# Hybrid S5 / conv / mLSTM layer on one core: the sixteen copies of the S5 inputs become steps of the S5 side job

## The chip, the cores and the metric

The kernel runs on 1 core of one Trainium2 chip. The metric is the device time of one execution in microseconds (us). The kernel before takes 1469.58 us (median of 3 runs, 1468.60 to 1469.86).

## What is computed

One layer of a diffusion backbone (`DEPTH = 1`) on 256 latent tokens with a prefix of 256 context tokens, both 2048 wide. Both streams are normalised and modulated, go through one input projection, and feed three groups of heads; their outputs are concatenated, projected and followed by a SwiGLU feed-forward block.

```python
hx = _rmsnorm(x, norm1_g[l]) * (1.0 + sc1_x) + sh1_x
hc = _rmsnorm(ctx, norm1_g[l]) * (1.0 + sc1_c) + sh1_c
zx = hx @ w_in[l] + b_in[l]
zc = hc @ w_in[l] + b_in[l]
s5_c, s5_x = s5_mixer(zc[..., OFF_S5:OFF_CONV], zx[..., OFF_S5:OFF_CONV], ...)
ml_c, ml_x = mlstm_mixer(zc, zx, ml_norm_g[l], need_ctx)
cv_x = conv_module(zx[..., OFF_CONV:OFF_Q], ...)
x = x + g1_x * (jnp.concatenate([s5_x, cv_x, ml_x], axis=-1) @ w_out[l])
hx2 = _rmsnorm(x, norm2_g[l]) * (1.0 + sc2_x) + sh2_x
x = x + g2_x * _swiglu(hx2, w_ffn_in[l], w_ffn_out[l])
```

The change concerns the input of `s5_mixer`. It has 32 groups of 16 channels, each with a state of 64 complex numbers, scanned along the tokens in both directions. The input is the S5 part of `zc` and `zx`, 512 channels by 512 tokens.

## The kernel before

**The main stream.** TensorE multiplies the weights of the input projection, the GLU, the output projection and the feed-forward block, one chunk after the other. A chunk is 8 weight tiles of 128 by 128 in fp32. SyncE fetches it (`raw`, line 259), ScalarE rounds it (`whi`, a CAST by `acopy`, line 201), and VectorE takes the rest (`wlo = raw - whi`, line 168). There are three buffers of each. A tile is used in three matmuls for each output (`mm3`: whi by high part, whi by low part, wlo by high part, line 208), so a chunk with one moving block of 256 tokens is 24 matmuls of 256 columns. The order of the tiles is fixed by `tile_order()`: S5 and the first K tiles, then the conv tiles (where the change acts), the other K tiles, V, Q, O, and so on.

**The side jobs.** All other work is written as generators which the class `Sched` steps between tiles. It holds three counters (`sc.pe`, `sc.dve`, `sc.act`), to which the helpers add an estimated cost; every 8 tiles `pump()` steps the ready job with the lowest priority number until VectorE or ScalarE is counted more than 3500 ns ahead of TensorE. A step may return a delay. The S5 job and the conv job have priority 3, the modulation job (`mod_job`: matrix-vector products with the `wm` weights, whose sums are `macc` and `mods`) 2, the gates of the mLSTM 1 and its heads 4. The framework then settles the order in which each engine gets its instructions, engine by engine, and adds the waits.

**The S5 job.** The four tiles of its input come out of the main stream as `zT` (channels by tokens). Sixteen copies (`s5_moves`, lines 773 to 781) bring them into chunk layout `U`: each copies 32 partitions by 512 elements, eight on ScalarE and eight on VectorE, alternating. They are issued in one block, ahead of the job (line 925). The job then runs 16 rounds. `prep(p)` builds the tables of round p: `Wb`, `Mb` and `cc` from the parameters, the rotation table `tab` on ScalarE, four transposes of `Wb` (line 839) whose result ScalarE copies to `Wi`, and 16 matmuls `Mb` by `Wb` whose result ScalarE copies to `M2`. `main5(p)` multiplies `U[:, p, :]` by `Wi`, rotates and scans on VectorE (`Vr`), forms `H1`, and multiplies `H1` by `Mb` and `U` by `M2`; VectorE adds the result into `U`. `prep(p + 1)` and `main5(p)` are interleaved step by step. After round 15 ScalarE applies the GELU to `U` (line 907), and 32 copies bring it into `gT`, sixteen of them on ScalarE.

**PSUM.** The main stream has three banks `m` and two banks `qk`. All side jobs and conv tile 0 share three banks `b` (`bbank`): a side job that needs a bank waits until the reader of its last use is done. Lines 992 and 994 are the transposes at the end of the gates job, line 749 those of the modulation sums, line 755 the sums of these on ScalarE, line 187 those on VectorE (`rsum`).

Of the kernel before, what the change touches and what calls it, by code (L numbers as in the profile page):

```python
# [150 lines left out]
def hybrid_layer_kernel(ctx: ExitStack, tc: tile.TileContext, xt, ctxt, wm1, wmr, wst, wg, bvrow, pvd, cstd, s5p, out):  # L151
# [6 lines left out]
    sc = Sched()  # L158


    def n_of(ap):
        n = 1
        for s in ap.shape[1:]:
            n *= s
        return n

    def tt(o, a, b, op):
        V.tensor_tensor(out=o, in0=a, in1=b, op=op)  # L168
        sc.dve += 62 + 1.05 * n_of(o)
# [8 lines left out]
    def stt(o, a, s, b, op0, op1):  # L178
        V.scalar_tensor_tensor(o, a, s, b, op0=op0, op1=op1)  # L179
        sc.dve += 62 + 1.05 * n_of(o)  # L180

    def vcopy(o, a):
        V.tensor_copy(o, a)
        sc.dve += 62 + 0.8 * n_of(o)
# [5 lines left out]
    def scan(o, d0, d1, init, op0, op1):  # L190
        V.tensor_tensor_scan(o, d0, d1, init, op0=op0, op1=op1)
        sc.dve += 62 + 1.05 * n_of(o)
# [7 lines left out]
    def acopy(o, a):  # L200
        S.copy(o, a)  # L201
        sc.act += 190 + 0.84 * n_of(o)

    def mm(o, l, r, start, stop, native=False, tp=None, sgc=False, pin=False):
        kw = {}
        if tp is not None:
            kw["tile_position"] = tp
        i = P.matmul(o, lhsT=l, rhs=r, start=start, stop=stop, skip_group_check=sgc, **kw)  # L208
        if pin:
            tc.keep_in_program_order(i)  # L210
        n = n_of(o)
        sc.pe += (max(n * 4, 512) if native else max(n, 256)) / 2.36 / (1 if tp is None else 4)
# [10 lines left out]
    def bbank():  # L223
        return bank("b", 3)

    def tmp(n=512):
        return sb.tile([128, 512], F32, name="tmp", tag="tmp", bufs=4)[:, :n]
# [9 lines left out]
    def pvc(name, i=0, n=None):  # L237
        a, w = PV[name]
        return pv[:, a + i:a + i + (n if n is not None else 1)]
# [374 lines left out]
    zT = pre.tile([128, 4, 512], F32, name="zT", tag="T1")  # L614
# [155 lines left out]


    U = pre.tile([128, 16, 128], F32, name="U", tag="U")
    def s5_moves():
        for s in range(4):
            for q in range(4):
                o = U[32 * s:32 * s + 32, q::4, :]
                i = zT[32 * q:32 * q + 32, :, s::4]
                if (s + q) % 2:
                    vcopy(o, i)
                else:  # L780
                    acopy(o, i)

    def s5_job():
        Wb = pre.tile([128, 2, 2, 4, 32], F32, name="Wb", tag="s5W")
# [70 lines left out]
        def main5(p):  # L855
            u0 = 2 * p
            Mb, Wi, M2, tab = P5.pop(p)
            ps = bbank()
            pv4 = ps.rearrange("p (u r k) -> p u r k", u=2, r=2)
            for d in range(2):  # L860
                r = U[:, p, :]
                if d:
                    r = r.rearrange("p (h k) -> p h k", h=2)[:, :, ::-1]
                for ri in range(2):
                    mm(pv4[:, d, ri, :], Wi[:, d, ri, :], r, True, True, native=True)
            Vr = pre.tile([128, 2, 2, 128], F32, name="Vr", tag="s5V")
            P2 = tmp().rearrange("p (u r k) -> p u r k", u=2, r=2)
            tt(Vr, pv4, tab[:, :, 0:1, :].to_broadcast([128, 2, 2, 128]), OP.mult)
            tt(P2, pv4[:, :, ::-1, :], tab[:, :, 1:2, :].to_broadcast([128, 2, 2, 128]), OP.mult)
            tt(Vr[:, :, 0, :], Vr[:, :, 0, :], P2[:, :, 0, :], OP.add)  # L870
            tt(Vr[:, :, 1, :], Vr[:, :, 1, :], P2[:, :, 1, :], OP.subtract)
            yield
            for d in range(2):
                for ri in range(2):
                    scan(Vr[:, d, ri, :], rho[:, u0 + d:u0 + d + 1].to_broadcast([128, 128]), Vr[:, d, ri, :],
                         0.0, OP.mult, OP.add)
            yield
            H1 = tmp(256).rearrange("p (u r k) -> p u r k", u=2, r=2)
            H2 = tmp(256).rearrange("p (u r k) -> p u r k", u=2, r=2)
            tt(H1, Vr[:, :, :, 63:127], tab[:, :, 0:1, 63:127].to_broadcast([128, 2, 2, 64]), OP.mult)  # L880
            tt(H2, Vr[:, :, ::-1, 63:127], tab[:, :, 1:2, 63:127].to_broadcast([128, 2, 2, 64]), OP.mult)
            tt(H1[:, :, 0, :], H1[:, :, 0, :], H2[:, :, 0, :], OP.subtract)
            tt(H1[:, :, 1, :], H1[:, :, 1, :], H2[:, :, 1, :], OP.add)
            yield S5_Y[3]
            ps = bbank()
            for d in range(2):
                for ri in range(2):
                    h = H1[:, d, ri, :]
                    mm(ps[:, 0:64], Mb[:, d, ri, (1 - d):(5 - d), :].rearrange("p s c -> p (s c)"),
                       h[:, ::-1] if d else h, d == 0 and ri == 0, False, native=True)  # L890
            mm(ps[:, 0:64], M2, U[:, p, 64:128], False, True, native=True)
            stt(U[:, p, 64:128], U[:, p, 64:128], pvc("dcol", p), ps[:, 0:64], OP.mult, OP.add)
            yield

        yield from prep(0)
        for p in range(16):
            a, b = main5(p), (prep(p + 1) if p < 15 else iter(()))
            live = [b, a]
            while live:
                for g in list(live):  # L900
                    try:
                        d = next(g)
                    except StopIteration:
                        live.remove(g)
                        continue
                    yield
# [3 lines left out]
        for hh in range(2):  # L910
            for j in range(4):
                for q in range(4):
                    o, i = gT[hh][32 * q:32 * q + 32, :, j::4], U[32 * j:32 * j + 32, q + 8 * hh:q + 8 * hh + 5:4, 64:128]
# [8 lines left out]
            tt(gs[:, 2 * hh:2 * hh + 2, 1, :], gT[hh], gs[:, 2 * hh:2 * hh + 2, 0, :], OP.subtract)  # L922
        s5o["gT"], s5o["gs"] = gT, gs

    s5_moves()
    s5o = {}
    s5j = sc.add(s5_job(), P_S5)


# [364 lines left out]
    i = 0  # L1294
# [114 lines left out]
```

## Time and profile before

| What | Value |
|---|---|
| median of 3 runs | 1469.58 us (1468.60 to 1469.86) |
| time of the profiled execution | 1469.76 us |
| its span, first to last instruction | 1468.0 us |
| TensorE busy | 1423.0 us, 97% of the span |
| VectorE, ScalarE, GpSimdE busy | 68%, 49%, 7% |
| mean granted clock of TensorE | 0.991 |
| chain that ended last, by engine | PE 87%, DVE 4%, ACT 3%, DMA 2%, issue 2% |

PE is TensorE, PEld its weight load, DVE is VectorE, ACT is ScalarE, POOL is GpSimdE and SP is SyncE. A row of a timeline has the start and the duration in us, the engine, the line, the operation and its tiles; "xN" counts records, and a square bracket gives the idle time before it and what ended that. A matmul with fp32 operands leaves two records. The shares are means over the span; what a stage loses is read from its own rows.

### The profile page before, as it was taken

To read this page: it belongs to the slowest core of one execution; us is meant where nothing else is said; L and a number is where in the kernel's file an instruction comes from. 1 tells how busy PE (TensorE), PEld (TensorE's weight loads), DVE (VectorE), ACT (ScalarE), POOL (GpSimd) and SP (SyncE) were. 2 spreads that over 40 slices of the span, in tenths; PEclk is the share of its full clock that TensorE was granted. 3 is DMA by queue.
4 is the path that set the end of the run, shared out by engine and by line. 5 is a ranking of instruction groups with operands and counts; after the bars stand their busy time and mean duration, and the time that the engine had idled before them with its cause. 6 is when DMAs were issued, how large, how long until landed. Compare 5 with 4: busy or idle time off the path is not lost.

```text
span 1468.0 us, 29243 instructions
## 1 busy us (share of the span) xinstructions
PE 1423.0 (97%) x11840; PEld 1335.7 (91%) x11840; DVE 1004.2 (68%) x1960; ACT 716.0 (49%) x1199; POOL 107.2 (7%) x207
## 2 busy tenths in 40 slices
PE   6999899999999999998999999999999999999996
PEld 3888788887878999998999999999999999999996
DVE  7655699998988787988776667555544554555554
ACT  4333786654656555545544444433444334443353
POOL 1221111110101011111010000000000000000000
PEclk9999999999999999999999999999999999999999
DMA  9997464443436576688477786555555555555553
GB/s 359 360 360 294 160 234 138 165 162 123 147 121 233 196 270 237 239 312 321 150 262 269 257 291 237 186 187 187 185 184 185 186 188 182 186 187 187 186 175 114
DMA packets 87943, 315.56 MB, mean 215 GB/s; under 512 B 10096, under 2 KB 10880, under 8 KB 87808
## 3 DMA queue, kind: packets, MB, share of 16 engines
q1 hardware_dynamic: 60912, 216.67, 42.9%
q0 software_dynamic: 26896, 97.02, 18.4%
q8 instruction: 93, 1.52, 0.4%
q14 instruction: 42, 0.34, 0.1%
HBM read 311.55 MB, written 2.10 MB: 214 GB/s over the span
## 4 chain that ended last, share of the span: by engine, by line
PE 87%; DVE 4%; ACT 3%; DMA 2%; issue 2%; SPq 0%; POOL 0%; DVEq 0%; POOLq 0%; ACTq 0%
PE ps_m L208 71%; PE ps_b L208 11%; PE ps_qk L208 4%; DMA wm<-in_wm_dram 1%; DVE tmp L168 1%; DMA tmp<-in_wg_dram 1%; DVE macc L179 1%; DMA raw<-in_wst_dram 1%; DVE wlo L168 1%; PE ps_b L839 0%; ACT whi L201 0%; ACT tmp L195 0%; ACT U L201 0%; PE ps_b L749 0%; DVE xres L168 0%
## 5 line engine op out<-in xcount | busy, mean ns | idle before, releaser
L168 DVE TENSOR_TENSOR wlo<-raw,whi 128x1024 fp32r<-128x1024 f32 x386 | 471.9, 1224 | 315.9 <-ACT whi L201 311.1
L201 ACT CAST whi<-raw 128x1024 fp32r<-128x1024 f32 x386 | 404.0, 1047 | 502.3 <-PE ps_m L208 355.9
L208 PE MATMUL ps_m<-h,whi 128*128 128x256 f32 x2624 | 469.9, 282 | 3.6 <-ACT h L195 3.6
L208 PEld LDWEIGHTS ps_m<-h,whi 128*128 128x128 f32 x2624 | 403.8, 189 | 4.0 <-ACT h L195 4.0
L208 PE MATMUL ps_m<-h,wlo 128*128 128x256 f32 x1312 | 369.6, 282 | 0.0
L208 PE MATMUL ps_m<-ffa,whi 128*128 128x256 f32 x1408 | 251.1, 281 | 0.0
L208 PEld LDWEIGHTS ps_m<-h,wlo 128*128 128x128 f32 x1312 | 247.5, 189 | 0.0
L208 PEld LDWEIGHTS ps_m<-ffa,whi 128*128 128x128 f32 x1408 | 215.7, 188 | 1.4 <-issue 1.2
L208 PE MATMUL ps_m<-ffa,wlo 128*128 128x256 f32 x704 | 197.3, 280 | 0.0
L208 PE MATMUL ps_m<-hx,whi 128*128 128x256 f32 x960 | 186.9, 290 | 5.5 <-ACT hx L195 3.6
L208 PEld LDWEIGHTS ps_m<-hx,whi 128*128 128x128 f32 x960 | 148.8, 190 | 24.7 <-issue 16.3
L179 DVE SCALAR_TENSOR_TENSOR macc<-wm,cs,macc 128x512 f32<-128x512 f32 x180 | 134.6, 748 | 6.8 <-ACT macc L195 5.1
L208 PE MATMUL ps_m<-hx,wlo 128*128 128x256 f32 x480 | 135.5, 283 | 0.4 <-DVE wlo L168 0.4
L208 PEld LDWEIGHTS ps_m<-ffa,wlo 128*128 128x128 f32 x704 | 132.2, 188 | 0.0
L331 POOL DMA_DIRECT2D wm<-in_wmr_dram x128 | 67.5, 528 | 606.8 <-DVE macc L179 429.8
L208 PEld LDWEIGHTS ps_m<-hx,wlo 128*128 128x128 f32 x480 | 90.9, 190 | 0.8 <-DVE wlo L168 0.8
L179 DVE SCALAR_TENSOR_TENSOR xres<-ps_m,mods,xres 128x256 f32<-128x256 f32 x96 | 46.1, 482 | 35.2 <-PE ps_m L208 35.0
L179 DVE SCALAR_TENSOR_TENSOR XB<-XB,pv 128x256 f32<-128x256 f32 x120 | 53.9, 481 | 0.6
L208 PE MATMUL ps_m<-hc,whi 128*128 128x256 f32 x256 | 52.9, 288 | 0.0
L208 PE MATMUL ps_m<-mixm,whi 128*128 128x256 f32 x256 | 47.0, 285 | 0.0
L208 PE MATMUL ps_m<-whi,hx 128*128 128x512 f32 x128 | 46.5, 400 | 0.0
L201 ACT CAST ffa<-tmp 128x256 fp32r<-128x256 f32 x44 | 17.7, 405 | 49.7 <-DVE tmp L168 49.7
(267 smaller groups left out, 1967.2 us busy)
## 6 DMA issues: line engine op xcount, KB each, us to landing
raw<-in_wst_dram SPq DMA_DIRECT2D x386, 512.0 KB, 3.5
wm<-in_wmr_dram POOLq DMA_DIRECT2D x128, 512.0 KB, 5.4
wm<-in_wm_dram POOLq DMA_DIRECT2D x32, 512.0 KB, 7.2
wmu<-in_wm_dram POOLq DMA_DIRECT2D x16, 512.0 KB, 7.2
wmt<-in_wm_dram POOLq DMA_DIRECT2D x7, 512.0 KB, 5.9
wm<-in_wm_dram SPq DMA_DIRECT2D x5, 512.0 KB, 10.2
xr<-in_xt_dram SPq DMA_DIRECT2D x4, 512.0 KB, 6.5
cr<-in_ctxt_dram SPq DMA_DIRECT2D x4, 512.0 KB, 9.0
```

The costliest lines, as they stand in the source:

```text
L168: V.tensor_tensor(out=o, in0=a, in1=b, op=op)
L179: V.scalar_tensor_tensor(o, a, s, b, op0=op0, op1=op1)
L201: S.copy(o, a)
L208: i = P.matmul(o, lhsT=l, rhs=r, start=start, stop=stop, skip_group_check=sgc, **kw)
L331: i = (q or nc.gpsimd).dma_start(wm[key], src)
```

## The change

The function `s5_moves`, which issued all sixteen copies, becomes the generator `s5_move(q)`. It issues the four copies of quarter q (the rounds p = q, q + 4, q + 8, q + 12 take their input from it), two on ScalarE and two on VectorE, adds 500 to the counter `sc.act` for each copy on ScalarE, and returns to the planner after each two copies. The S5 job runs quarter 0 ahead of `prep(0)`, and quarters 1, 2 and 3 ahead of rounds 0, 1 and 2. Lines of the S5 job stand two lower in the kernel after, later ones four lower.

```diff
--- before.py
+++ after.py
@@ -770,15 +770,17 @@
 
 
     U = pre.tile([128, 16, 128], F32, name="U", tag="U")
-    def s5_moves():
+    def s5_move(q):
         for s in range(4):
-            for q in range(4):
-                o = U[32 * s:32 * s + 32, q::4, :]
-                i = zT[32 * q:32 * q + 32, :, s::4]
-                if (s + q) % 2:
-                    vcopy(o, i)
-                else:
-                    acopy(o, i)
+            o = U[32 * s:32 * s + 32, q::4, :]
+            i = zT[32 * q:32 * q + 32, :, s::4]
+            if (s + q) % 2:
+                vcopy(o, i)
+            else:
+                acopy(o, i)
+                sc.act += 500
+            if s % 2:
+                yield
 
     def s5_job():
         Wb = pre.tile([128, 2, 2, 4, 32], F32, name="Wb", tag="s5W")
@@ -892,8 +894,11 @@
             stt(U[:, p, 64:128], U[:, p, 64:128], pvc("dcol", p), ps[:, 0:64], OP.mult, OP.add)
             yield
 
+        yield from s5_move(0)
         yield from prep(0)
         for p in range(16):
+            if p < 3:
+                yield from s5_move(p + 1)
             a, b = main5(p), (prep(p + 1) if p < 15 else iter(()))
             live = [b, a]
             while live:
@@ -922,7 +927,6 @@
             tt(gs[:, 2 * hh:2 * hh + 2, 1, :], gT[hh], gs[:, 2 * hh:2 * hh + 2, 0, :], OP.subtract)
         s5o["gT"], s5o["gs"] = gT, gs
 
-    s5_moves()
     s5o = {}
     s5j = sc.add(s5_job(), P_S5)
```

The instructions of the kernels are the same in number and kind but for two table loads on ScalarE fewer; their order differs. Until conv tile 0 has begun (some 151 us in the trace of before) and from 600 us on, each engine has the same order in both. Three places between follow.

The first is ScalarE at the beginning of the conv tiles. Before, the one copy and the block of seven copies to `U` stand ahead of the CASTs of the weight chunks:

```order
L201 COPY U_1768<-zT_1744 32x4x128
L195 ACTIVATE kT_1749<-ps_b_221,bks_1750 128x512
L195 ACTIVATE kT_1749<-ps_b_222,bks_1750 128x512
L201 COPY U_1768<-zT_1744 32x4x128 x7
L201 CAST whi_1818<-raw_1786 128x1024
L201 CAST whi_1866<-raw_1816 128x1024
L201 COPY Mb_1833<-tmp_1922 64x20x16
L201 CAST whi_1896<-raw_1864 128x1024
L195 ACTIVATE tmp_1932<-cst_68,s5c_215 128x128
```

After, the copies are spread. The row `Wi` is the copy that frees the PSUM bank of the first four transposes of `Wb`, and `M2` the one behind the first `Mb` by `Wb` matmuls; this is what stands ahead of them:

```order
L195 ACTIVATE cc_2020<-bc_2002 128x2x16
L195 ACTIVATE cc_2020<-bc_2002 128x64
L201 COPY U_1768<-zT_1744 32x4x128
L195 ACT_TABLE_LOAD
L195 ACTIVATE tab_1889<-tmp_1890 128x2x128
L195 ACTIVATE tmp_1891<-tmp_1890 128x256
L201 CAST whi_1926<-raw_1852 128x1024
L195 ACTIVATE tab_1889<-tmp_1891,kc_70 128x2x128
L201 CAST whi_1998<-raw_1924 128x1024
L201 COPY Wi_1938<-ps_b_1939 128x512
L201 COPY U_1768<-zT_1744 32x4x128 x3
L201 COPY M2_1945<-ps_b_1946 128x128
```

Two CASTs now stand ahead of the six last copies, and those copies ahead of the later CASTs, of `Wi` and of `M2`. VectorE's eight copies stay one block at their place.

The second is VectorE in the gates job, from the first scans of the forget gate to the row that the gate transposes (line 992, after: 996) read. Before:

```order
L191 SCALAR_TENSOR_TENSOR tmp_2894<-kc_70,tmp_2892 32x256 x4
L168 TENSOR_TENSOR wlo_3116<-raw_2967,whi_3114 128x1024
L168 TENSOR_TENSOR rows_2839<-rows_2839,tmp_2894 64x512
L168 TENSOR_TENSOR tmp_2984<-tmp_2984,tmp_2985 128x256
L173 TENSOR_SCALAR rows_2839<-rows_2839,tmp_2894 32x256 x2
L191 SCALAR_TENSOR_TENSOR tmp_2893<-kc_70,tmp_2894,rows_2839 32x256 x2
L191 SCALAR_TENSOR_TENSOR tmp_2893<-kc_70,tmp_2893,rows_2839 32x256 x2
L179 SCALAR_TENSOR_TENSOR XB_1755<-XB_1755,pv_64 128x256
L173 TENSOR_SCALAR tmp_2893<-tmp_2893 64x256
L179 SCALAR_TENSOR_TENSOR XB_1755<-XB_1755,pv_64 128x256
L168 TENSOR_TENSOR rows_2839<-tmp_2893,tmp_2894 64x256
```

After, with a step of the modulation job next to it; the row `mods` frees the PSUM bank of a modulation sum:

```order
L191 SCALAR_TENSOR_TENSOR tmp_2801<-kc_70,tmp_2799 32x256 x4
L179 SCALAR_TENSOR_TENSOR XB_1755<-XB_1755,pv_64 128x256
L168 TENSOR_TENSOR rows_2773<-rows_2773,tmp_2801 64x512
L179 SCALAR_TENSOR_TENSOR XB_1755<-XB_1755,pv_64 128x256
L173 TENSOR_SCALAR rows_2773<-rows_2773,tmp_2801 32x256 x2
L191 SCALAR_TENSOR_TENSOR tmp_2800<-kc_70,tmp_2801,rows_2773 32x256 x2
L191 SCALAR_TENSOR_TENSOR tmp_2800<-kc_70,tmp_2800,rows_2773 32x256 x2
L168 TENSOR_TENSOR tmp_2830<-tmp_2830,tmp_2831 128x256
L173 TENSOR_SCALAR tmp_2800<-tmp_2800 64x256
L187 TENSOR_REDUCE mods_1759<-ps_b_2936 128x4
L168 TENSOR_TENSOR rows_2773<-tmp_2800,tmp_2801 64x256
```

The sum of the modulation job stands behind the second scans, and on TensorE the transposes of the gates, which in the kernel after take the bank that this sum reads, stand behind it.

The third is ScalarE at the end of the S5 job, where the V tiles end and the Q tiles begin (`RH` is the Q tile with its bias that the heads need). Before:

```order
L201 CAST whi_5475<-raw_5429 128x1024
L195 ACT_TABLE_LOAD
L195 ACTIVATE U_1768<-U_1768 128x16x64
L201 COPY gT_5336<-U_1768 32x128 x8
L201 COPY gT_5337<-U_1768 32x128 x8
L201 CAST whi_5505<-raw_5473 128x1024
L201 CAST gs_5400<-gT_5336 128x2x256
L201 CAST gs_5400<-gT_5337 128x2x256
L201 CAST whi_5537<-raw_5503 128x1024
L201 CAST whi_5575<-raw_5535 128x1024
L195 ACTIVATE RH_5471<-ps_m_5472,pv_64 128x256
```

After:

```order
L201 CAST whi_5532<-raw_5481 128x1024
L195 ACT_TABLE_LOAD
L195 ACTIVATE U_1768<-U_1768 128x16x64
L755 ACTIVATE macc_4921,mods_1759<-ps_b_5487 128x128
L201 COPY gT_5382<-U_1768 32x128 x8
L201 COPY gT_5383<-U_1768 32x128 x8
L755 ACTIVATE macc_4921,mods_1759<-ps_b_5487 128x128
L201 CAST gs_5446<-gT_5382 128x2x256
L201 CAST gs_5446<-gT_5383 128x2x256
L755 ACTIVATE macc_4921,mods_1759<-ps_b_5487 128x128 x2
L195 ACTIVATE RH_5479<-ps_m_5480,pv_64 128x256
L195 ACTIVATE macc_5497<-wm_5281,cs_104 128x512
```

Before, the last matmuls of round 15 (`U` by `M2`) stand 21 matmuls ahead of the end of the V tiles on TensorE; after, they stand two matmuls ahead of it. The GELU, the copies to `gT` and the CASTs to `gs` now stand between the CAST of the third chunk of Q (`whi_5532`) and `RH`, with the CASTs of the fourth and fifth chunk behind `RH`. Before, the CASTs of three more chunks stood ahead of `RH`.

## Rows read from the trace of the kernel before

**Rows 1.** waits of TensorE, 140 to 450 us: us, times, longest

```profile
PE ps_b L208 <- ACT whi L201: 4.1, 1, 4.1
```

**Rows 2.** the timeline of TensorE, 155 to 182 us

```profile
159.23 0.80 PE L208 MATMUL ps_b<-hx,whi 128*128 128x256 f32 x2 [4.07 <-ACT whi L201]
...
171.38 1.06 PE L208 MATMUL ps_b<-wm,cs 128*32 128x512 f32 x6
172.38 0.66 PE L839 MATMUL ps_b<-cst,Wb 128*128 128x128 f32 x4
172.96 0.89 PE L208 MATMUL ps_b<-Mb,Wb 128*32 128x128 f32 x32
...
174.12 1.05 PE L208 MATMUL ps_b<-U,Wi 128*128 128x128 f32 x8
...
181.70 1.08 PE L208 MATMUL ps_b<-tmp,Mb 128*128 128x64 f32 x8
```

**Rows 3.** the timeline of ScalarE, 146 to 176 us

```profile
150.29 7.82 ACT L201 COPY U<-zT 32x512 f32<-32x512 f32 x7
158.14 1.99 ACT L201 CAST whi<-raw 128x1024 fp32r<-128x1024 f32 x2
...
163.23 1.28 ACT L195 ACT_TABLE_LOAD   x1
...
173.07 0.59 ACT L201 COPY Wi<-ps_b 128x512 f32<-128x512 f32 x1 [0.64 <-PE ps_b L839]
173.88 0.27 ACT L201 COPY M<-ps_b 128x128 f32<-128x128 f32 x1 [0.22 <-PE ps_b L208]
```

**Rows 4.** windows: length, busy times, then the granted clock

```profile
158.00:159.00 1.00, 0.00 (x0) 0.00 (x0) 0.00 (x0) 0.97 (x2) 0.00 (x0) 0.50 0.00 0
160.15:167.10 6.95, 6.95 (x38) 5.29 (x37) 3.48 (x5) 6.50 (x13) 0.00 (x0) 0.72 0.66 225
245.00:250.00 5.00, 5.00 (x30) 4.80 (x30) 4.87 (x10) 2.51 (x5) 0.00 (x0) 0.66 0.18 71
450.00:455.00 5.00, 3.42 (x22) 2.83 (x23) 5.00 (x8) 1.48 (x3) 0.53 (x1) 1.00 0.55 181
```

**Rows 5.** the timeline of VectorE, 146 to 184 us

```profile
147.58 5.00 DVE L183 COPY U<-zT 32x512 f32<-32x512 f32 x8 [1.78 <-ACT zT L195]
```

**Rows 6.** the timeline of TensorE, 229 to 245 us

```profile
231.49 1.12 PE L208 MATMUL ps_b<-rows,XB 32*128 32x512 f32 x2
...
244.02 0.30 PE L992 MATMUL ps_b<-cst,rows 64*128 64x64 f32 x2 [1.44 <-DVE rows L168]
```

**Rows 7.** the timeline of VectorE, 232 to 252 us

```profile
238.26 0.69 DVE L179 SCALAR_TENSOR_TENSOR tmp<-tmp 64x512 f32<-64x512 f32 x1 [0.83 <-ACT tmp L195]
...
239.27 2.75 DVE L191 TENSOR_TENSOR_SCAN tmp<-kc,tmp 32x256 f32<-32x256 f32 x4
...
244.88 3.06 DVE L191 TENSOR_TENSOR_SCAN tmp<-kc,tmp,rows 32x256 f32<-32x256 f32 x4
```

**Rows 8.** the timeline of ScalarE, 434 to 458 us

```profile
439.13 1.06 ACT L195 ACTIVATE U<-U 128x1024 f32<-128x1024 f32 x1 [0.45 <-DVE U L179]
440.22 6.88 ACT L201 COPY gT<-U 32x128 f32<-32x128 f32 x16
...
448.08 1.14 ACT L201 CAST gs<-gT 128x512 fp32r<-128x512 f32 x2
...
451.02 0.47 ACT L195 ACTIVATE RH<-ps_m,pv 128x256 f32<-128x256 f32 x1
```

**Rows 9.** the timeline of TensorE, 436 to 456 us

```profile
443.37 0.40 PE L208 MATMUL ps_m<-hx,whi 128*128 128x256 f32 x2
...
449.06 0.40 PE L208 MATMUL ps_m<-hx,whi 128*128 128x256 f32 x2
451.16 0.51 PE L208 MATMUL ps_m<-hx,whi 128*128 128x256 f32 x2 [1.71 <-ACT whi L201]
...
453.08 0.39 PE L208 MATMUL ps_m<-hx,wlo 128*128 128x256 f32 x1 [0.41 <-DVE wlo L168]
```

## The prediction

> **What bounds the kernel now.** I read the table of busy shares first: TensorE is busy for 97% of the span, and the chain that ended last is matmuls for 87% of it. A change of order can therefore win only time in which TensorE stands still or runs at a low clock. Then the view of waits for the stretch in which the two orders differ, some 150 to 600 us. Its one large entry is a wait for a rounded weight chunk, `whi` [rows 1]. The reader is to see that it happens once.
>
> The timeline of TensorE puts it at the first conv tile: a stop of 4.07 us until 159.23, hence from 155.16 [rows 2]. The timeline of ScalarE shows the cause: from 150.29 seven copies to `U` run for 7.82 us, 1.12 each, and only behind them, at 158.14, come the two CASTs [rows 3]. The window view adds a second loss: during the stop the granted clock falls to .50, which is the lower of the two levels, 1.2 GHz instead of 2.4, and between 160.15 and 167.1 it is still .72 on the mean [rows 4]. What that cost: a full chunk on 256 tokens is 24 matmuls, and two of them took 449.06 - 443.37 = 5.69 us, so 2.85 each and .119 a matmul [rows 9]. From 159.23 to 171.38 TensorE did 70 such matmuls (by the order; 8.3 us) and one of the four matmuls of a modulation step (.27 of the 1.06 in rows 2), 8.6 us of work in 12.15 us. So 3.6 us went into the low clock and the split step, and the whole place loses 4.1 + 3.6 = 7.7 us.
>
> **The change at the conv tiles.** The copies cost what they cost; eight stay with VectorE, as one block of 5.00 us at the same place [rows 5], where nothing waits for them. On ScalarE the first chunk's CAST now stands behind one copy of the later seven: 150.29 + 1.12 + 1.0 = 152.4, ahead of the 155.1 at which TensorE asks. The old stop is gone. The question is what is late next.
>
> TensorE then does, by its new order, the chunk (2.85), a modulation step (1.06), the four transposes of `Wb` (172.38 to 172.96: .58) and 7 matmuls (.83), and is at 160.4 at the `Mb` by `Wb` matmuls. These need a bank of the group `b`, and the three are held by conv tile 0, the modulation sum and the transposes just made. The last is freed by ScalarE's copy `Wi`. Ahead of `Wi` in ScalarE's queue, from 150.29 on, stand four copies to `U` (4 x 1.12 = 4.5), four CASTs (4 x 1.0 = 4.0), a table load (1.28) and the ten short steps which in before fill 160.15 to 167.1: 6.50 busy there, less two CASTs and the load, 3.1 [rows 3, 4]. That is 12.9 us, so `Wi` begins at 163.2 and ends .59 later, at 163.8. TensorE waits 3.4 us, where before it waited for nothing at that copy.
>
> Behind `Wi` stand three more copies and then `M2`, ready at 163.8 + 3.35 + .27 = 167.4. The matmuls `U` by `Wi` wait for its bank. TensorE reaches them after .9 for `Mb` by `Wb` [rows 2] and 17 matmuls (2.0), at 166.7: .7 more. So 4.1 us of stops replace 4.1. What can be won is clock. A stop of 3.4 us isn't in the trace; the nearest, of 4.07, cost 3.6 us of slowness, the one of 1.71 at 451.16 [rows 9] nothing (clock 1.00 in 450 to 455, rows 4). Between 0 and 3.6 I take 1.8, since a part of slow work is hidden by the wait for `M2` behind it. New loss 5.9, old loss 7.7: **-1.8 us**, bounds -3.6 and 0.
>
> **The gates.** Before, the `selg` matmuls end at 231.49 + 1.12 = 232.6, which I call T, and the transposes of the gates wait 1.44 us [rows 6]. In the new order TensorE has between the two 66 matmuls (7.85), transposes, `Mb` by `Wb` and `U` by `Wi` (.6 + .9 + 1.0), four transposes of a modulation sum (.6) and a modulation step (1.06): it is there at T + 12.0. Their bank comes free when VectorE has read the modulation sum, and that row stands behind the second scans. Before, the first step of the forget gate begins at 238.26 = T + 5.7 and the second scans end at 244.88 + 3.06 = T + 15.3 [rows 7]. In the new order a `wlo` (1.1) and a short step (.3) between them are gone, two conv steps (.8) are added, and two short ones and the reading follow (.7): T + 15.4. The wait is 3.4 instead of 1.4: **+2.0 us**. The clock drop behind it (.66 in 245 to 250, rows 4: 1.7 us) is there before and stays; a second one is the upper bound, +3.7, and the lower one is 0, if conv steps move out of VectorE's way in time.
>
> **The end of the S5 job.** Here ScalarE must do, after round 15, the GELU (1.06), sixteen copies to `gT` (6.88) and two CASTs to `gs` (1.14) [rows 8]. Before, round 15 ended some 5 us ahead of the end of the V tiles, and TensorE had two and more chunks cast in advance; it lost 1.71 + .41 us [rows 9]. In the new order round 15 ends with the V tiles (443.37 in before; I call it V). Then ScalarE has a CAST which waits for V itself (1.05), a table load (1.28), the GELU, the sixteen copies, the `gs` CASTs, four short readings (1.0 by my estimate, the size of a CAST) and only then `RH` (.47): V + 12.9. TensorE has three chunks and four transposes, 3 x 2.85 + .6: at V + 9.2 it stands before the matmuls that need `RH`. Wait 3.7. Then the next two chunks' CASTs, which before stood ahead of `RH`, end at V + 14.5 and V + 15.5; with the few matmuls between, about 1.2 more. Sum 4.9 against 2.1: +2.8. The clock: as above, 0 to 3.6, and I take 1.8. **+4.6 us**, bounds +1 (if the table load and the CAST are over before the GELU's input is there) and +7.
>
> The modulation steps also run some ten steps further ahead, and two of thirty table loads go (1.28 each; I count nothing for them, since no wait of TensorE in this stretch ends with a row behind a table load but those worked out here). From 600 us on the order is the same. Added waits elsewhere between 230 and 430 us: VectorE is nearly full there, but TensorE lost nothing to it; 0 to 2 us, I take 0.
>
> Sum: 1469.76 (the profiled execution; its span of 1468.0 and 1.8 around it) - 1.8 + 2.0 + 4.6 = 1474.6. That execution was .2 above the median, so **1474.4 us**.
>
> **A rule against the row.** The clock fell in the 4.07 us stop, not at 1.71 us, and it fell also after the stop of 1.44 us in the gates, where TensorE had done small matmuls before. The length of the stop alone doesn't decide it here. The Trainium skill (TensorE: Matmul & The Clock Gate, HAM oscillation) says that an idle gap of enough length puts the clock back, and that this is paid anew at each gap. By that rule the full price stands at each of the three new stops; the trace agrees at one and leaves the others open.
>
> **The rivals.**
> - *The stop simply goes.* If ScalarE reaches `Wi`, and later `RH`, ahead of TensorE, only the 7.7 us remain: 1469.6 - 7.7 = 1461.9. For it: the copies are the only cause of the large wait. Against it: the queue of ScalarE as added up is longer than TensorE's work by 3.4 and 3.7 us, and the durations would have to be off by a quarter. With one of the two new stops it is about 1466.
> - *The clock holds.* The new stops come, but are short enough for the full clock: -3.6 + 2.0 + 2.8 = +1.2, so 1470.8. For it: 1.71 us cost nothing. Against it: they are nearer to 4.07.
> - *Each stop brings the full drop.* 1.8 more at the conv tiles, 1.7 at the gates, 1.8 at the end of S5: 1474.4 + 5.3 = 1479.7. It decides from the point where TensorE stands for some 3.4 us.
>
> **Chances.** The forecast, 1472.6 to 1478: .50. Each stop with the full drop, above 1478: .17. The clock holds or gains and losses cancel, 1466.7 to 1472.5: .18. The stop simply goes, wholly or in part: .15. About .2%, 2.9 us, is what a measurement here can tell from no change. So faster .15, same .18, slower .67. The range takes in the partly faster case and nearly all of the slow one: 1465 to 1480.5; the forecast's own is 1472.6 to 1478.
>
> **What would show it.** Right: no wait for `whi` at 155 us, but one of about 3.4 us on `Mb` by `Wb` for ScalarE's `Wi`; about 3.4 us at the transposes of the gates, for VectorE's modulation sum; 3 to 5 us at the first `RH` matmuls, with clocks under 1.00 behind the first and the last. Wrong: `Wi` done before TensorE asks, or the end of round 15 well ahead of the V tiles' end.

## The result, and the profile after

The kernel after takes 1478.78 us (median of 4 runs, 1477.43 to 1480.23), the kernel before 1469.09 us in the same comparison. The ratio is 1.0068 (95% interval 1.005 to 1.0085): 9.7 us slower (7.3 to 12.5 by the interval), where 4.8 had been forecast (1474.4 us against a median of 1469.58). 1478.78 lies just above the forecast's own range, which ended at 1478. The profiled execution took 1478.43 us, with a span of 1476.7 us and a mean granted clock of 0.986, against 1469.76, 1468.0 and 0.991.

The view of TensorE's waits in the kernel after, 140 to 610 us (us in total, times, longest); its five largest rows, against [rows 1]:

```profile
PE ps_qk L208 <- ACT RH L195: 3.7, 1, 3.7
PE ps_b L208 <- ACT Wi L201: 3.2, 1, 3.2
PE ps_b L996 <- DVE mods L187: 3.1, 1, 3.1
PE ps_b L208 <- DVE tmp L168: 2.0, 4, 0.7
PE ps_m L208 <- DVE wlo L168: 1.7, 2, 1.1
```

The 4.1 us for `whi` are gone. Three waits of over 3 us stand in their place, each for the row that the prediction named, and some short ones. TensorE's timeline shows where:

```profile
162.42 0.86 PE L208 MATMUL ps_b<-Mb,Wb 128*32 128x128 f32 x32 [3.21 <-ACT Wi L201]
...
244.00 0.46 PE L996 MATMUL ps_b<-cst,rows 64*128 64x64 f32 x4 [3.05 <-DVE mods L187]
...
459.05 2.08 PE L208 MATMUL ps_qk<-RH,kT 128*128 128x256 f32 x4 [3.65 <-ACT RH L195]
...
463.87 0.58 PE L208 MATMUL ps_m<-hx,wlo 128*128 128x256 f32 x1 [1.09 <-DVE wlo L168]
```

**The conv tiles.** ScalarE's timeline, against [rows 3]:

```profile
149.67 1.05 ACT L201 CAST whi<-raw 128x1024 fp32r<-128x1024 f32 x1
...
151.64 1.12 ACT L201 COPY U<-zT 32x512 f32<-32x512 f32 x1
...
154.67 1.15 ACT L201 COPY U<-zT 32x512 f32<-32x512 f32 x1
...
156.35 1.13 ACT L201 COPY U<-zT 32x512 f32<-32x512 f32 x1
157.50 1.28 ACT L195 ACT_TABLE_LOAD   x1
...
160.77 1.03 ACT L201 CAST whi<-raw 128x1024 fp32r<-128x1024 f32 x1
161.71 0.57 ACT L201 COPY Wi<-ps_b 128x512 f32<-128x512 f32 x1
162.30 3.45 ACT L201 COPY U<-zT 32x512 f32<-32x512 f32 x3
165.78 0.27 ACT L201 COPY M<-ps_b 128x128 f32<-128x128 f32 x1
```

The first CAST is there at 150.7, long before TensorE asks. Three copies, the table load, three more CASTs and short steps between them then keep `Wi` back until 162.3, and TensorE stands for 3.21 us.

**The gates.** VectorE's timeline, against [rows 7]:

```profile
240.16 3.05 DVE L191 TENSOR_TENSOR_SCAN tmp<-kc,tmp,rows 32x256 f32<-32x256 f32 x4
...
243.59 0.28 DVE L173 TENSOR_SCALAR tmp<-tmp 64x256 f32<-64x256 f32 x1
243.79 0.16 DVE L187 TENSOR_REDUCE mods<-ps_b 128x4 f32<-128x16 f32 x1
```

The reading of the modulation sum (`mods`, .16 us long) stands behind the second scans, and the transposes of the gates begin as it ends, after a wait of 3.05 us. Before, they waited 1.44 us [rows 6].

**The end of S5.** ScalarE's timeline, against [rows 8]:

```profile
446.14 1.05 ACT L201 CAST whi<-raw 128x1024 fp32r<-128x1024 f32 x1 [5.65 <-PE ps_qk L208]
447.21 1.28 ACT L195 ACT_TABLE_LOAD   x1
448.50 1.06 ACT L195 ACTIVATE U<-U 128x1024 f32<-128x1024 f32 x1
...
449.72 6.84 ACT L201 COPY gT<-U 32x128 f32<-32x128 f32 x16
...
456.99 1.12 ACT L201 CAST gs<-gT 128x512 fp32r<-128x512 f32 x2
...
458.52 0.47 ACT L195 ACTIVATE RH<-ps_m,pv 128x256 f32<-128x256 f32 x1
...
459.49 2.94 ACT L201 CAST whi<-raw 128x1024 fp32r<-128x1024 f32 x3
```

The V tiles end at about 446.1, where the CAST that waits for them begins; `RH` ends 12.9 us later, and ScalarE is busy all the time between.

The windows view (length, busy time of PE, PEld, DVE, ACT and POOL with counts, then the granted clock) shows the second part of the cost, against [rows 4]:

```profile
160.00:165.00 5.00, 2.58 (x41) 2.43 (x42) 2.45 (x2) 4.95 (x7) 0.00 (x0) 0.85 0.90 306
...
245.00:250.00 5.00, 5.00 (x30) 4.79 (x28) 5.00 (x13) 1.76 (x4) 0.00 (x0) 0.66 0.29 105
455.00:460.00 5.00, 1.35 (x4) 1.02 (x4) 1.73 (x4) 4.93 (x15) 0.00 (x0) 0.71 0.00 0
460.00:465.00 5.00, 3.91 (x13) 2.68 (x12) 3.72 (x6) 4.28 (x6) 0.75 (x2) 0.50 0.34 116
465.00:470.00 5.00, 5.00 (x35) 5.00 (x35) 3.59 (x6) 1.70 (x4) 0.83 (x2) 0.77 0.89 280
```

With each of the three waits TensorE's clock falls to the lower level (a granted clock of .50, 1.2 GHz): behind the first for 3.4 us (from 163.5), behind the second for 3.4 us (from 245.4), and at the end of S5 for the longest time, from 457.06, in the middle of the wait, for 10.2 us. The low stretch of the gates stood there before as well [rows 4]; it is as long as it was, though the wait ahead of it grew from 1.44 to 3.05 us.

To compare whole kernels I add up two things for each trace between 150 and 1450 us: the gaps between TensorE's matmuls, and half of the time at the low clock (what a busy TensorE loses in it; a gap inside it is so counted in both). The last column is the rest of the span: work, and what lies ahead of 150 us and behind TensorE's end.

| kernel | ratio to before (95%) | span, us | gaps | half of low clock | span less both |
|---|---|---|---|---|---|
| before | 1 | 1468.0 | 16.9 | 6.8 | 1444.3 |
| after | 1.0068 (1.0050 to 1.0085) | 1476.7 | 20.8 | 11.9 | 1444.0 |
| m2_bank | 1.0073 (1.0047 to 1.0098) | 1475.5 | 18.7 | 11.9 | 1444.9 |
| gate_bank | 1.0050 (1.0033 to 1.0067) | 1474.2 | 18.6 | 8.5 | 1447.1 |
| late_gelu | 1.0047 (1.0033 to 1.0061) | 1474.8 | 20.1 | 8.5 | 1446.2 |
| three_fixes | 1.0021 (1.0010 to 1.0033) | 1469.0 | 16.4 | 5.1 | 1447.5 |
| no_count | 0.9999 (0.9989 to 1.0009) | 1466.9 | 17.5 | 5.1 | 1444.3 |
| no_count_m2_bank | 0.9995 (0.9985 to 1.0005) | 1467.3 | 15.6 | 5.1 | 1446.6 |
| no_count_m2_late | 1.0000 (0.9990 to 1.0009) | 1465.4 | 17.4 | 5.1 | 1442.9 |
| count_250 | 1.0047 (1.0030 to 1.0064) | 1472.8 | 18.8 | 10.2 | 1443.8 |
| count_alone | 1.0036 (1.0023 to 1.0049) | 1470.6 | 20.6 | 6.8 | 1443.2 |
| block_vector_late | 0.9999 (0.9989 to 1.0008) | 1465.6 | 16.4 | 3.4 | 1445.8 |
| spread_vector | 0.9966 (0.9954 to 0.9979) | 1461.4 | 15.4 | 3.4 | 1442.6 |
| spread_vector_late | 0.9949 (0.9934 to 0.9963) | 1458.0 | 12.3 | 3.4 | 1442.3 |

All but the ratios are of one execution each. The last column varies by some 5 us, so single profiles tell 2 or 3 us apart only by their rows, and the ratios decide. That the low clock belongs to the kernels, and not to the profiled execution alone, shows in the mean granted clock of all executions: .986 to .988 in the four of the kernel after, .988 to .994 in the 66 of the kernel before that were timed beside the experiments. By the means of these, .987 and .990, the low clock has a part of up to 4 us in the loss (an estimate: the missing share of the clock times the span, 19.2 less 14.9 us).

### The profile page after: what moved, and what is told of

It reads as the page before. It is cut to its first block, busy times and chain, and to the rows that moved or that the text cites. A ratio compares the mean times of both kernels' runs of the same rounds, so it can differ in the third digit from the quotient of the medians.

```text
span 1476.7 us, 29212 instructions
## 1 busy us (share of the span) xinstructions
PE 1429.0 (97%) x11840; PEld 1340.5 (91%) x11840; DVE 1002.4 (68%) x1960; ACT 713.0 (48%) x1197; POOL 107.5 (7%) x207
## 4 chain that ended last, share of the span: by engine, by line
PE 78%; DVE 8%; ACT 5%; DMA 4%; issue 4%; POOL 1%; SPq 0%; DVEq 0%; ACTq 0%; POOLq 0%
PE ps_m L208 64%; PE ps_b L208 9%; PE ps_qk L208 4%; DMA raw<-in_wst_dram 2%; DVE macc L179 1%; DVE tmp L168 1%; DVE wlo L168 1%; ACT tmp L195 1%; ACT whi L201 1%; DMA tmp<-in_wg_dram 1%; DMA wmu<-in_wm_dram 1%; POOL wm L331 0%; ACT gT L201 0%; DVE Vr L168 0%; DMA bc<-in_s5p_dram 0%
## 5 line engine op out<-in xcount | busy, mean ns | idle before, releaser
L208 PEld LDWEIGHTS ps_m<-hx,whi 128*128 128x128 f32 x960 | 150.6, 192 | 22.2 <-issue 15.6
```

## The experiments

**Do the three places carry the loss?** Each of the first three kernels is the kernel after with one place mended.

m2_bank:

```diff
-            ps = bbank()
+            ps = bbank() if p else qbank()   # bank of the Mb by Wb matmuls
```

> The kernel after, with one edit: the PSUM bank of the first Mb by Wb matmuls comes from the group qk, which is idle there, not from b. Theory (three places, each with its own wait on an engine's queue): the 3.21 us wait of TensorE for the copy Wi at 159.2 and the 3.4 us at the low clock behind it (1.7 us of work) go; part returns at H1, which VectorE makes. 2 to 5 us under the kernel after, and the other two waits (3.05 us in the gates, 3.65 us before RH) stay. Rival (the side jobs as a whole stand in a worse order, single waits only pass the loss on): within 1 us of the kernel after.

1.0073: no gain. The wait for `Wi` is gone and two others have taken its place, as this view of m2_bank shows (140 to 180 us):

```profile
PE ps_b L208 <- DVE tmp L168: 1.9, 1, 1.9
PE ps_m L208 <- DVE wlo L168: 1.7, 1, 1.7
```

VectorE comes late with `wlo` of the next chunk (1.7) and with `H1` (the row `tmp`, 1.9), 3.6 us in all for 3.2, and the low stretch of 3.4 us comes behind these. The rival was right here: at the conv tiles the wait only changes its name.

gate_bank:

```diff
         yield 8000
-        ps = bbank()
+        ps = qbank()
```

> The kernel after, with one edit: the bank of the transposes of the gates comes from the group qk, not from b, so that they need not wait for VectorE's reading of the modulation sum. Theory: the 3.05 us wait at 241 us goes, and with it the low clock from 245.4 on (3.4 us, 1.7 us of work): 3 to 5 us under the kernel after. Rival (bank is not the reason, the rows themselves come late from VectorE, or the loss is passed on): the wait stays over 2 us, or the time stays within 1 us.

1.0050, .0018 or 2.6 us less than after by the two ratios, whose intervals overlap. In its trace, 230 to 260 us:

```profile
PE ps_b L208 <- DVE tmp L168: 1.3, 1, 1.3
PE ps_qk L996 <- DVE rows L173: 0.7, 1, 0.7
PE ps_qk L996 <- DVE rows L168: 0.6, 1, 0.6
```

The forecast was 3 to 5 us. The transposes wait 1.3 us, now for their own rows, and TensorE waits 1.3 us for an `H1`; but no stretch at the low clock is left here. So the bank was the reason for the wait of 3.05 us, of which some .5 was to be won. In this trace the clock was the larger part (1.7 us); how much of the 2.6 us is its doing is open, since the same wait in m2_bank's trace (3.07 us) goes with a low stretch of 6.8 us.

late_gelu:

```diff
+        yield 20000
         act(U[:, :, 64:128], U[:, :, 64:128], AF.Gelu_apprx_tanh)
```

> The kernel after, with one edit: the S5 job returns a delay of 20000 ns of TensorE's counter ahead of the GELU, so that ScalarE has a CAST and two of the sixteen gT copies ahead of RH instead of all sixteen. Everything up to the end of the V tiles stays. Theory: the wait of 3.65 us for RH, the 1.09 us behind it and most of the 10.2 us at the low clock (3.6 us of work) go: 5 to 8 us under the kernel after, unless the copies come in the way of the heads later. Rival (the copies have to be done anyway and ScalarE hands the loss on): within 1.5 us of the kernel after, with new waits for RH or whi between 460 and 500 us.

1.0047, .0021 or 3.1 us less than after, where 5 to 8 had been forecast; the intervals overlap. Its waits, 440 to 500 us:

```profile
PE ps_b L208 <- DVE RH L168: 2.1, 1, 2.1
```

The wait for ScalarE's `RH` is away, the low clock shrinks from 10.2 to 3.4 us, and 2.1 us come back later in the first head, where TensorE waits for VectorE. It is the theory with a part of the rival.

three_fixes has the three edits together.

> The kernel after with the three edits of m2_bank, gate_bank and late_gelu together. Theory (three separate places): the gains add, the wait for Wi, the one for the modulation sum and the one for RH are all away; by the ratios of the single edits (1.0073, 1.005 and 1.0047 against 1.0068 of the kernel after) 1.0030 to 1.0045 against the kernel before, so some 3 to 5 us of the 10 are back. Rival (the loss of the kernel after lies in the order as a whole, and the places only show it): it stays at 1.0047 or above.

1.0021: .0047 of .0068 are back, a little more than forecast, and clear of the kernel after. The single edits sum to .0034, so the places add up within the intervals. They don't bring back the whole: waits of 1.7 and 1.9 us for VectorE at the conv tiles and of 2.1 us in the first head are left.

**Spreading, or the counter?** The change has two parts: the copies become steps, and each adds 500 ns to the planner's counter of ScalarE. no_count drops the second:

```diff
                 acopy(o, i)
-                sc.act += 500
```

> The kernel after without the 500 ns that each copy adds to ScalarE's counter. The order is the same up to the second round of S5, so the wait for Wi stays; at the end of S5 the last U by M2 matmul stands 30 matmuls ahead of the end of V instead of 2, and two CASTs stand ahead of RH's copies. Theory: the Wi wait of 3.2 us stays, the RH wait shrinks by 3 us or more with its low clock: 3 to 7 us under the kernel after. Rival (spreading the copies is itself the loss, wherever S5 ends): within 2 us of the kernel after.

0.9999. This is the experiment that decides: without one line the whole loss is gone (some 10 us, where 3 to 7 had been forecast), with the copies spread as in the change. Its order at the conv tiles is that of after, and its trace has the same wait of 3.2 us for `Wi`, one of 1.6 for `M2` with it. Rows of TensorE's timeline, and windows:

```profile
165.10 0.86 PE L208 MATMUL ps_b<-Mb,Wb 128*32 128x128 f32 x32 [3.22 <-ACT Wi L201]
...
168.69 1.16 PE L208 MATMUL ps_b<-U,Wi 128*128 128x128 f32 x8 [1.60 <-ACT M L201]
```

```profile
160.00:165.00 5.00, 1.88 (x19) 1.29 (x11) 1.72 (x2) 4.95 (x9) 1.05 (x2) 1.00 0.72 243
165.00:170.00 5.00, 3.30 (x51) 2.95 (x52) 0.84 (x2) 3.60 (x4) 0.00 (x0) 1.00 0.79 248
```

No low stretch follows these two waits (clock 1.00 in both windows), while the one wait of 3.21 us in after was followed by 3.4 us of it. At full clock TensorE reaches `U` by `Wi` sooner and waits for `M2` instead: from `Mb` by `Wb` to `U` by `Wi` it takes 3.59 us here and 4.36 in after (162.42 to 166.78). So of the 1.7 us that the low clock cost there only .8 show. What differs in favour of no_count comes later: the gates, and above all the end of S5. ScalarE's timeline of no_count:

```profile
437.78 1.06 ACT L195 ACTIVATE U<-U 128x1024 f32<-128x1024 f32 x1 [3.22 <-DVE U L179]
438.93 1.05 ACT L201 CAST whi<-raw 128x1024 fp32r<-128x1024 f32 x1
439.88 6.85 ACT L201 COPY gT<-U 32x128 f32<-32x128 f32 x16
446.75 1.05 ACT L201 CAST whi<-raw 128x1024 fp32r<-128x1024 f32 x1
...
450.78 1.05 ACT L201 CAST whi<-raw 128x1024 fp32r<-128x1024 f32 x1 [1.94 <-PE ps_m L208]
453.75 0.47 ACT L195 ACTIVATE RH<-ps_m,pv 128x256 f32<-128x256 f32 x1 [1.92 <-PE ps_m L208]
```

The GELU begins at 437.8, since round 15 ended well ahead of V, and `RH` waits for TensorE (1.92 us), not TensorE for `RH`. TensorE's one wait there is for VectorE's `vx` (the V tiles for the heads), 1.8 us, with 3.4 us at the low clock behind it. The transposes of the gates wait for nothing.

count_alone does the other half: the kernel before, its block of copies kept, with the 500 ns for each.

```diff
                     acopy(o, i)
+                    sc.act += 500
```

> The kernel before with one part of the change alone: each of the eight copies on ScalarE, still in one block, adds 500 ns to ScalarE's counter. Theory now (the counter, not the spreading, is what costs): the order changes all the way to 600 us, the last U by M2 matmul stands 12 matmuls ahead of the end of V, and RH stands behind the sixteen gT copies, two gs CASTs, four readings and a macc step: a wait of 3 us or more at RH, 4 to 10 us slower than before. Rival (the spreading costs, the counter only in company with it): within 2 us of before.

1.0036, 5 us slower than before without moving a copy out of the block. The size was as expected, the place was not. The interval lies below that of the kernel after, so the count alone makes about half of the loss; spreading alone (no_count) makes none, and the other half comes when both are there. Two views of its waits, 140 to 180 us and 430 to 480 us:

```profile
PE ps_b L208 <- ACT whi L201: 4.7, 1, 4.7
...
PE ps_b L749 <- DVE macc L179: 3.4, 1, 3.4
```

`RH` was not waited for; the beginning of Q waits 3.4 us for a modulation sum on VectorE, and the old stop at the conv tiles is 4.7 instead of 4.1 us.

count_250 halves the amount (`sc.act += 250`).

> The kernel after with 250 instead of 500 ns for each copy. If the size of the count is what costs, half of the loss goes (about 5 us under the kernel after). If the count only tips the planner into another order, the time goes by that order: here the end of S5 is as in the kernel after (3 matmuls ahead of the end of V, RH behind the sixteen copies), so 1.005 to 1.009 against before, and only the middle differs.

1.0047. The order at the end of S5 is that of after, and the waits are the same to .1 us (3.18 for `Wi`, 2.97 in the gates, 3.62 for `RH`). So the amount is not a price that each copy pays: it tips the planner, and 250 tips it nearly as 500 does. The ratio alone would not show this, for it lies just under the 1.005 expected of the same order, and half of the loss (1.0034) is inside its interval of 1.0030 to 1.0064. The two profiles differ by 3.9 us; their low stretches at 700 us and at the end, which vary between executions of the same order, are 3.4 and 8.5 us long here against 6.8 and 11.3 in after.

**Is there a version that beats both?** no_count_m2_bank joins two of the edits above.

> The kernel after without the counter's 500 ns and with the qk bank for the first Mb by Wb matmuls. Theory: the waits for Wi (3.2 us) and M2 (1.6 us) of no_count go, up to 3.5 us come back at wlo and H1 as in m2_bank; CASTs of three chunks stand ahead of RH, so no wait of 3 us there. 0 to 4 us under the kernel before. Rival: the edit shifts later steps, so that a new wait takes the gain, and the time is within 1 us of before or above it.

0.9995, no difference: the 3.2 us appear again one row later (`U` by `Wi`, which needs the same copy), and Q's beginning waits 2.8 us for `wlo`. The theory had overlooked that `Wi` is needed for itself too. no_count_m2_late adds the delay of the GELU:

> no_count_m2_bank with the GELU delayed by 20000 ns. Theory: the CASTs of two more chunks stand ahead of the last gT copies and of RH, so that the wait of 2.8 us at wlo at the beginning of Q shrinks to 1 us or less: 1 to 3 us under no_count_m2_bank, 1 to 4 us under before. Rival: the copies come in the heads' way, no gain.

1.0000. At `wlo` .7 us are left of 2.8 as expected, but 1.7 us come back at the first head and 2.2 instead of .4 in the GLU behind. The rival was right.

If ScalarE's queue is what is too long at the conv tiles, copies should leave it. spread_vector makes all sixteen on VectorE (.6 us each there, 1.1 on ScalarE), without the counter; spread_vector_late delays the GELU too. block_vector_late keeps the block of the kernel before, with twelve of sixteen on VectorE.

```diff
-            if (s + q) % 2:
-                vcopy(o, i)
-            else:
-                acopy(o, i)
-                sc.act += 500
+            vcopy(o, i)
```

> The kernel after, but all sixteen copies are made by VectorE, nothing is added to ScalarE's counter, and the S5 job delays its GELU by 20000 ns as in late_gelu. Theory (ScalarE's queue at the conv tiles is what TensorE waits for, VectorE has room there): no wait for whi at 155 us and none over 1 us for Wi; some 3.7 us more on VectorE bring a wait of 0 to 2 us at wlo or H1; seven gT copies stand ahead of RH, so 1 to 2 us there. 2 to 7 us under the kernel before. Rival (the planner's order as a whole decides, and each edit draws a new one): within 2 us of before, with other waits of the same sum.

> The kernel before, the copies still in one block, but twelve on VectorE and four on ScalarE, and the GELU delayed by 20000 ns. Theory: ScalarE is free for the CAST some 4.5 us earlier, so the wait of 4.07 us for whi goes; VectorE's block becomes about 7.4 us, so up to 1 us at wlo. All sixteen gT copies still stand ahead of RH, and S5 ends behind the end of V: 3 us or more there. 0 to 4 us under the kernel before. Rival as above: within 1 us of before or slower.

> spread_vector_late without the delay of the GELU: all sixteen copies on VectorE as steps of the S5 job. The last U by M2 matmul stands 5 matmuls behind the end of V and RH stands behind all sixteen gT copies, as in the kernel after. Theory: the conv tiles stay as in spread_vector_late (no wait for whi, about 0.9 us at wlo), and at RH a wait of 2 us or more comes back, with a low clock if it is 3 us or more: 2 to 7 us over spread_vector_late, so 0.996 to 1.000 against before. Rival (the delay does nothing, the vector copies are the whole gain): within 1.5 us of spread_vector_late.

spread_vector_late takes 1460.60 us, 0.9949 of before: the fastest here, 7.5 us under before where 2 to 7 had been forecast. spread_vector takes 1462.54 (0.9966), block_vector_late 1467.64 (0.9999, where 0 to 4 us less than before had been forecast). The waits of spread_vector_late, 140 to 610 us, and windows of it:

```profile
PE ps_b L208 <- ACT Wb L201: 1.8, 3, 1.1
PE ps_m L208 <- DVE wlo L168: 1.2, 2, 0.7
PE ps_b L208 <- DVE mods L187: 0.9, 1, 0.9
```

```profile
155.00:160.00 5.00, 4.12 (x34) 2.94 (x33) 4.90 (x8) 4.08 (x6) 1.05 (x2) 1.00 0.42 121
160.00:165.00 5.00, 5.00 (x68) 4.68 (x68) 4.06 (x8) 0.27 (x1) 0.00 (x0) 1.00 0.95 344
```

No wait is over 1.2 us, and there is no low stretch between 150 and 680 us. VectorE is busy for 4.90 of 5 us where the copies are, and TensorE loses .9 us to it. Against spread_vector the delay is worth some 2 us (the intervals just overlap): without it Q begins with a wait of 2.4 us, for `wlo` and not for `RH` as expected, and a low stretch of 3.4 us follows, though the expectation had one only from 3 us on. block_vector_late lost its stop at the conv tiles (1.6 us in two pieces are left) and has no low stretch between 150 and 690 us either, and yet gained nothing, with 2.4 us at `wlo` and 1.3 in the GLU. spread_vector against no_count (0.9966 and 0.9999) differs in the engine of eight copies alone; but the planner draws another order from that too, and no run separates the engine from the order.

## Why the prediction was right, and where it was off

**The sign and the steps held.** The stop for `whi` went. TensorE waited 3.21 us for `Wi` (forecast 3.4), 3.05 for the modulation sum (3.4), 3.65 for `RH` (3.7) and 1.09 at the chunks behind it (1.2). `RH` came 12.9 us after V as added up. Only the .7 us for `M2` did not show: TensorE ran at the low clock there and came late itself. In no_count, at full clock, it waited 1.6 us for `M2`, so this link of the chain was there too. Adding the durations in the order of one engine's queue up to the row that frees the bank gave the three large waits within .4 us.

**The sum was half of what came.** The time fell not into the forecast's own range, with its chance of .50, but just above it, into the band of the full drop at each stop (.17). The loss can be read between two matmuls of the main stream that both kernels have: one ahead of the conv tiles, which begins at 146.10 us before and at 144.32 after, and the last of the input projection, at 581.75 and 590.34. The stretch takes 435.7 us before and 446.0 after, 10.4 more. From there to TensorE's end both take 875 us. With the 1.8 us by which this execution of after was ahead at the first of the two, these are the 8.7 us between the profiles. What the gaps and the low clock (half of TensorE's busy time in it) make of the 10.4:

| place | forecast, us | gaps | clock |
|---|---|---|---|
| conv tiles, to 230 us | -1.8 | +.8 | -.7 |
| gates, 230 to 260 us | +2.0 | +1.6 | 0 |
| between, 260 to 440 us | 0 | +.8 | 0 |
| end of S5, from 440 us | +4.6 | +2.6 | +3.6 |
| sum | +4.8 | +5.8 | +2.9 |

The other 1.7 us lie in TensorE's busy time; their cause is open. The gaps came near the forecast, which had 4.8 us of them as well, with the clock at -1.8 and +1.8. Two terms were mis-sized.

**The clock at the end of S5.** I took 1.8 us for it, the middle of 0 and 3.6. The trace has 10.2 us at the low level, less 3.1 us of gaps in them: 7.1 us of work at half speed, 3.6 lost. This is the upper bound of the forecast and in part chance: m2_bank and count_250 have 10.2 us as well, but gate_bank, with the same wait of 3.65 us, has 6.8.

**The gain at the conv tiles was not there.** I forecast -1.8. Gaps grew by .8 (a wait of .5 us for `kT` and smaller ones), the loss by clock went from 2.4 to 1.7. The 3.6 us that the sum gave to the slowness of the old stop were too many: 4.83 us of TensorE's time lay in the low stretch, which is 2.4 lost, and some .7 of the rest lies in the modulation step that was split there. Its one matmul ahead was counted with .27 us, a quarter of the step, and took 1.85 us at half speed. It is no quarter: [rows 2] shows the other three of the four in 1.06 us (two records each), and in after all four take 1.07.

**What the sum had not.** The .8 us of waits between 260 and 440 us, where it took 0. From the GLU on it counted nothing, and this came out, but by two changes against each other. Before, TensorE waits twice in the GLU, at 585 and 589 us:

```profile
PE ps_m L208 <- ACT RH L195: 1.6, 1, 1.6
PE ps_m L208 <- ACT tmp L195: 1.2, 1, 1.2
```

After, these are gone, and 1.3 us of other gaps come up to 690 us (rows of `mixc`, a modulation sum, the second norm). Against this gain of some 1.4 us stand the low stretches at 700 us and at the end, which are 6.8 and 11.3 us long instead of 3.4 and 8.9. The length of these two varies between traces that have the same order there (3.4 or 6.8, and 8.5 to 11.8), so that part is not shown to belong to the change.

**The cause lay one step deeper than the rows.** The prediction named the order at three places, and mending them returned .0047 of .0068. But it took the order as given by the spreading of the copies. no_count and count_alone show that it takes the counter: without the 500 ns the spreading costs nothing, and the 500 ns alone cost half. `acopy` counts 190 + .84 x 512 = 620 ns for a copy of 512 columns; with the 500 it is 1120, which is what the trace has (7.82 us for seven). So the planner was told the truth, and with ScalarE counted busier it ran the steps of S5 later: the last `U` by `M2` stands 2 matmuls ahead of the end of V, without the count 30.

**The rivals.** *The stop simply goes* fell with the wait for `Wi`; *the clock holds* fell with the low stretches; *each stop brings the full drop* is nearest to the time measured (1479.7), though not by its own mechanism: the drop was full at the end of S5 alone, and the traces bear out no length of a stop from which it comes (3.22 us in no_count without a low stretch, 1.44 us in [rows 6] with one). The rule of the Trainium skill cited there (TensorE: Matmul & The Clock Gate, HAM oscillation) agrees with the trace of after as far as each of the three waits had a low stretch of its own; the trace of no_count, with 3.22 us and none, does not agree.

## What to carry to other kernels

When work moves from one place of an engine's queue to another, list what stands behind it until the next row that TensorE or a PSUM bank waits for; at the three places here the wait was a plain sum of durations, put on paper to within .4 us. What such a wait costs in clock was not to be had so: the forecast was 0 for it, and about 3 us came. A short row that frees a bank can hold TensorE for far longer than it runs (.57 us for `Wi` and .16 for the modulation sum, waits of 3.21 and 3.05). That ordering it first would pay is not shown: taking the bank out of its way won nothing at the conv tiles and 2.6 us, not clear of noise, in the gates. And treat an estimate in a planner as part of the schedule: a truer number is another order, to be timed like any other edit, one part at a time. The fastest version here gave the copies to the engine with room, as steps; part of them in one block there won nothing.

## What the runs showed that was not expected

The price of a wait in clock is not fixed by its length. A wait of 3.55 us for `h` (ScalarE), at some 680 to 700 us, stands in all fourteen traces: in eight with 3.4 us at the low level, in six with 6.8. The wait for `RH` of 3.65 us goes with 10.2 us in after and 6.8 in gate_bank, that of 3.05 in the gates with 3.4 in after and 6.8 in m2_bank. The 3.2 us for `Wi` were followed by 3.4 in after and by none in no_count; the 2.4 us at the beginning of Q were followed by 3.4 in spread_vector and by none in block_vector_late. So single traces do not price the clock; the executions together do. Nor is a trace without low stretches the same as a fast kernel: between 150 and 680 us spread_vector_late (0.9949) has none, and block_vector_late (0.9999) has none either.
